# One pace instead of two for the loads of the modulation weights in the first FFN

## The chip, the cores and the metric

The kernel runs on one core of a Trainium2 chip. The metric is the device time of one execution in microseconds; the median of several executions is given. The engines are named as in the profile: PE (matrix products), DVE (vector work), ACT (activations and copies), POOL (general work) and SP, which here only issues DMA transfers. Each engine works through its own queue in order.

## The reference, cut to what matters

Two layers of a diffusion backbone run over 256 latent tokens and, as far as they are needed, 256 context tokens; the model width is 1024 and the FFN width 2816. Each sub-layer computes `x <- LayerNorm(alpha*x + w*gate*f(x*(1+scale)+shift))`. The FFN is `(silu(h@Wa) * (h@Wu)) @ Wout`. Shift, scale and gate come from nine "modulation" vectors a layer:

```python
m  = (silu(c)     @ ada_w[i] + ada_b[i])   # 9 vectors of 1024 for the latent tokens
mc = (silu(c_ctx) @ ada_w[i] + ada_b[i])   # the same for the context tokens
```

Layer 0 is FFN, neighbourhood attention, FFN; layer 1 is FFN, short convolution, FFN. All is float32.

## The kernel before, in words

Every weight matrix is loaded in units of 512 KB (256 rows by 512 columns), and each unit is split into a high part (ACT copy, line 205) and a low part (DVE subtraction, line 208). Each product is made of three matmuls (high by high, low by high, high by low), which are float32r and 512 columns wide.

The first FFN of layer 0 runs over latent and context tokens together (512 columns). Its 2816 hidden columns are worked in three parts (`parts`, of 4, 4 and 3 panels of 256). In each part come first the panels (`f0_mm`, lines 615 to 617, then silu, product and a split in `f0_gate`, lines 621, 622, 110 and 111), and then the second product of that part (`out_gemm` over `ffn_w_out`, lines 162 to 165), whose results are added to x by `residual` (lines 366 to 373).

Beside it, as background, the kernel computes the modulation vectors that later sub-layers need. `ada` loads the weights in chunks of 128 rows by 1024 columns (512 KB, line 285, three buffers `ar`) and DVE multiplies each by the conditioning column and accumulates (first chunk of a vector line 276, the others line 278). A group has two accumulators `acc` of 1024 columns, and there are two such buffers, so that the accumulation of the next group can begin only when PE has read the accumulators of the group before. PE sums over the partitions with four small matmuls (line 309), DVE adds the bias (line 310), and the rows go to DRAM (line 312). Groups 1 to 3 accumulate one vector for both kinds of tokens: 8 chunks, each used twice (four DVE instructions a chunk). Groups 4 to 7 hold two vectors for the latent tokens: 16 chunks, each used once (two DVE instructions).

`ada` is a generator: one call of it (`bg_step`) issues one chunk with its accumulation, or one of the four steps that close a group (bias, two empty ones, the small matmuls). Groups 1 to 3 so take 12 calls each, and groups 4 to 7 take 20; the small matmuls fall on the calls 12, 24, 36, 56, 76, 96 and 116. The calls are dealt out by `tick`: the rate `background[1]` is added at every tick, and each whole one is a call. A tick is six wide matmuls of PE. The first part of the FFN has 40 ticks of panels after the background is set up (rate 0.45) and 32 of second product, the second part 64 and 32, the third part 48 and 24.

The order of PE's instructions is the order of the program, written out by hand. For the other engines a list scheduler decides the order ahead of the run: by priority (place in the program, moved forward by 40 for the weight splits and back by `ADA_LATE` = 20 for the background from the second part's second product on), and by when it expects data and buffers. On the chip each queue then runs in that fixed order.

Of the kernel before, what the change touches and what calls it, by code (L numbers as in the profile page):

```python
# [68 lines left out]
def backbone_kernel(  # L69
# [23 lines left out]
    def nm(s):  # L93
        uid[0] += 1
        return f"{s}_{uid[0]}"
# [7 lines left out]
    def mmb(s="mm", t=0):  # L103
        return bank("at" if t % 2 else "mm", s)
# [11 lines left out]
    background = [None, 0.0, 0.0]  # L116
# [19 lines left out]
    def bg_step():  # L136
        with tc.high_priority(offset=-ada_late[0]):
            if next(background[0], 0) == 0:
                background[0] = None

    def tick(n=1):
        clock[0] += n
        for w in [w for w in waiting if w.due <= clock[0]]:
            w.get()
        background[2] += background[1] * n
        while background[0] is not None and background[2] >= 1:
            background[2] -= 1
            bg_step()
# [186 lines left out]
    def fold_cols(l, v, m, ln):  # L335

        r = sm.tile([32, P], F32, tag="mrow", bufs=2, name=nm("mrow"))
        for i, src in enumerate((scr[l][v, (m + 1) * D:(m + 2) * D], scr[l][v, m * D:(m + 1) * D],
                                 ln_g[ln[0], ln[1]], ln_b[ln[0], ln[1]])):
            sync.dma_start(r[8 * i:8 * i + 8], src.rearrange("(a b) -> a b", b=P))  # L340

        def rest():
            ps = tpb("mcT")
            nc.tensor.transpose(ps[:, 0:32], r, ident[0:32, 0:32])
            c = sm.tile([P, 6, KC], F32, tag="gcol", bufs=2, name=nm("gcol"))
            nc.vector.tensor_copy(c[:, 0:4].rearrange("p a b -> p (a b)"), ps[:, 0:32])
            nc.vector.scalar_tensor_tensor(out=c[:, 4], in0=c[:, 0], scalar=1.0, in1=c[:, 2], op0=ALU.add, op1=ALU.mult)
            nc.vector.scalar_tensor_tensor(out=c[:, 5], in0=c[:, 0], scalar=1.0, in1=c[:, 3], op0=ALU.add, op1=ALU.mult)
            nc.vector.tensor_tensor(out=c[:, 5], in0=c[:, 5], in1=c[:, 1], op=ALU.add)
            return c[:, 4], c[:, 5]  # L350

        return Late(6, rest)
# [9 lines left out]
    def residual(ps, xt, gate, wgt, alpha, stats=None, behind=()):  # L362

        t = sp.tile([P, 512], F32, tag="tmp", bufs=3, name=nm("res"))[:, 0:ps.shape[1]]
        with queued(behind[0:1]):
            nc.vector.scalar_tensor_tensor(out=t, in0=ps, scalar=wgt, in1=gate, op0=ALU.mult, op1=ALU.mult)
        with queued(behind[1:2]):
            if alpha is None:
                nc.vector.tensor_tensor(out=xt, in0=xt, in1=t, op=ALU.add)
            else:  # L370
                nc.vector.scalar_tensor_tensor(out=xt, in0=xt, scalar=alpha, in1=t, op0=ALU.mult, op1=ALU.add)
            if stats is not None:
                nc.vector.bn_stats(stats, xt)

    def stat_tile(n=2):
        return sm.tile([P, 3, 6], F32, tag="stats", bufs=6, name=nm("st"))[:, 0:n]

    def finish_stats(st):
        mv = sm.tile([P, 2], F32, tag="mv", bufs=6, name=nm("mv"))
        norm_ins[:] = [nc.vector.bn_aggr(mv, st)]  # L380
        rs = sm.tile([P, 1], F32, tag="rs", bufs=6, name=nm("rs"))
        nc.gpsimd.tensor_tensor(out=rs, in0=mv[:, 1:2], in1=lnc[:, 0:1], op=ALU.add)
        nc.gpsimd.tensor_tensor(out=rs, in0=rs, in1=lnc[:, 1:2], op=ALU.pow)
        return mv, rs
# [5 lines left out]
    def modulated(z, mv, rs, GB, lag, ahead=False):  # L390

        for h in range(2):
            norm_ins[1:] = [nc.vector.tensor_scalar(z[h], z[h], mv[:, 0:1], rs, op0=ALU.subtract, op1=ALU.mult)]

        def rest():
            G, B = GB.get()
            res = []
            for h in range(2):
                ps = tpb("hT")
                for k in range(4):  # L400
                    nc.tensor.transpose(ps[:, k * P:(k + 1) * P], z[h][:, k * P:(k + 1) * P], ident)
                t = sp.tile([P, 512], F32, tag="s2", bufs=S2, name=nm("h"))
                with tc.high_priority(offset=LN_EARLY):
                    hi, lo = act(F32R, "hTh"), act(F32R, "hTl")
                    for k in range(4):
                        s, c = slice(k * P, (k + 1) * P), slice(4 * h + k, 4 * h + k + 1)
                        nc.scalar.activation(t[:, s], ps[:, s], AF.Identity, bias=B[:, c], scale=G[:, c])
                    ins = split(t, hi, lo)
                res.append((hi, lo))
            if ahead:  # L410
                fence[:] = [i.ins for i in ins]
            return res

        return Late(lag, rest)
# [33 lines left out]
    def run(gen):  # L448
        for _ in gen:
            pass  # L450
# [159 lines left out]
    def f0_mm(ps, units, j, z, ks):  # L610
        s = slice(z * 256 + j * P, z * 256 + (j + 1) * P)
        for k in ks:
            hi, lo = units[k // UK]
            lh, ll = hi[:, k % UK, s], lo[:, k % UK, s]
            nc.tensor.matmul(ps, lh, hT0[k][0], start=(k == 0), stop=False)  # L615
            nc.tensor.matmul(ps, ll, hT0[k][0], start=False, stop=False)  # L616
            nc.tensor.matmul(ps, lh, hT0[k][1], start=False, stop=(k == KC - 1))  # L617

    def f0_gate(bk):
        t = sp.tile([P, 512], F32, tag="s2", bufs=S2, name=nm("sil0"))  # L620
        nc.scalar.activation(t, bk[0], AF.Silu)
        nc.vector.tensor_tensor(out=t, in0=t, in1=bk[1], op=ALU.mult)
        hi, lo = act(F32R, "gh"), act(F32R, "gl")
        split(t, hi, lo)
        return hi, lo

    def w1(p, us=range(KU)):
        return [wpair(w_in, u, p * 256, FF + p * 256, "w1") for u in us]
# [28 lines left out]
    for fh, (p0, p1) in enumerate(parts):  # L657
        gT = []
        for p in range(p0, p1):
            units = u0 if p == 0 else u1 if p == 1 else w1(p)  # L660
            for j in range(2):
                if p == 0:
                    bk = b0[j]
                elif p == 1 and j == 0:
                    bk = b1
                else:
                    bk = []
                    for z in range(2):
                        bk.append(mmb("f0", z))
                        for k in range(0, KC, 2):  # L670
                            f0_mm(bk[z], units, j, z, (k, k + 1))
                            tick()
                gT.append(f0_gate(bk))
        if fh == 0:
            for v in range(2):
                big = hp.tile([P, 2, 512], F32, tag="pt", bufs=4, name=nm("gate"))
                sync.dma_start(big.rearrange("p a b -> p (a b)"),
                               bass.AP(scr[0].tensor, scr[0][v, 2 * D:3 * D].offset, [[0, P], [1, D]]))
                gates.append([big[:, 0], big[:, 1]])
            background[1] = 0.44  # L680
        elif fh == 1:
            background[1] = 0.64
            ada_late[0] = ADA_LATE

        def evac(t, n, bank, fh=fh):
            if fh < 2:
                residual(bank, xt[t][n], gates[t // 2][n], 0.5, None if fh else ALPHA)
                return
            if n == 0:
                stats[t] = stat_tile()  # L690
            residual(bank, xt[t][n], gates[t // 2][n], 0.5, None, stats[t][:, n])
            if n == 1:
                mv, rs = finish_stats(stats[t])
                hTs[t] = modulated(xt[t], mv, rs, GB[t // 2], F0_LAG[t])

        if fh == 2:
            while made[0] < 5:
                bg_step()
            GB = [fold_cols(0, v, 3, (0, 0)) for v in range(2)]
        nk = 2 * (p1 - p0)  # L700
        order = [(t, n, u) for n in range(2) for t in range(4) for u in range(nk // UK)]
        run(out_gemm(w_out, lambda k, t: (gT[k][0][:, t * P:(t + 1) * P], gT[k][1][:, t * P:(t + 1) * P]),
                     nk, order, evac, "w2", wrow0=p0 * 256))
# [454 lines left out]
```

## Time and profile before

| | us |
|---|---|
| median of 3 executions | 1268.82 |
| the three executions | 1268.34, 1268.82, 1272.64 |
| the profiled execution | 1273.84 |
| its span, from first to last instruction | 1272.0 |
| PE busy in it | 1246.2 |
| DVE busy | 954.9 |
| ACT busy | 590.2 |
| mean granted TensorE clock | 0.995 |

The span is the time between the first and the last instruction that the profiler shows; the execution's own time is 1.84 us longer. PE's busy share is not the same as PE at its peak, but idle time of PE is time in which the program's longest engine did nothing. [...]

### The profile page before, as it was taken

The numbers are of one execution on the slowest core, as the hardware profiler recorded it, in microseconds if no ns is written. First come the engines' busy times: TensorE is split into PE (matmuls) and PEld (weight loads), VectorE is DVE, ScalarE is ACT, GpSimd is POOL, SyncE is SP. The second block draws the span as 40 slices with busy tenths as digits, with TensorE's granted clock in tenths as the row PEclk, the third lists the DMA queues.
The fourth block names the chain that finished last, engine by engine and source line by source line (L and its number), as shares of the span: only waits on it lengthen the run. The fifth ranks groups of instructions, "written<-read, shape, count | busy, mean of one in ns | idle before, by whom it ended". The sixth has DMA issues, their size and how long they took to land.

```text
span 1272.0 us, 17236 instructions
## 1 busy us (share of the span) xinstructions
PE 1246.2 (98%) x5890; PEld 1007.0 (79%) x5890; DVE 954.9 (75%) x1681; ACT 590.2 (46%) x1148; POOL 42.3 (3%) x71
## 2 busy tenths in 40 slices
PE   7999999999999999989999999999999999999997
PEld 5787778788768878767888788888788887888786
DVE  3699887688878867888898646997646787977545
ACT  2432132412315556577755435645435744655431
POOL 0000000000001111111000000000000000000000
PEclk9999999999989999999999999999999999999999
DMA  9877578587862654554899745798645764786641
GB/s 298 297 230 244 177 239 296 162 303 246 287 212 67 196 123 79 108 128 123 274 310 333 236 148 182 253 325 286 228 146 170 234 213 133 256 285 187 222 155 54
DMA packets 202712, 268.59 MB, mean 211 GB/s; under 512 B 30026, under 2 KB 149298, under 8 KB 202624
## 3 DMA queue, kind: packets, MB, share of 16 engines
q1 hardware_dynamic: 202624, 267.49, 66.3%
q8 instruction: 46, 0.75, 0.2%
q14 instruction: 42, 0.34, 0.1%
HBM read 265.27 MB, written 2.17 MB: 210 GB/s over the span
## 4 chain that ended last, share of the span: by engine, by line
PE 88%; DVE 4%; DMA 3%; ACT 3%; issue 1%; POOL 0%; SPq 0%; DVEq 0%; ACTq 0%; POOLq 0%
PE w L162 17%; PE w L165 17%; PE w L163 17%; PE f L615 6%; PE f L616 6%; PE f L617 6%; PE wc L162 2%; PE wc L165 2%; PE wc L163 2%; PE wkv L162 2%; PE wkv L163 2%; PE wkv L165 2%; PE gT L467 1%; DMA bias<-in_na_rpb_dram 1%; DMA w1r<-in_ffn_w_in_dram 1%
## 5 line engine op out<-in xcount | busy, mean ns | idle before, releaser
L205 ACT ACTIVATE w1h<-w1r 128x512 fp32r<-128x512 f32 x348 | 199.8, 624 | 172.8 <-PE w L165 51.8
L208 DVE TENSOR_TENSOR w1l<-w1r,w1h 128x512 fp32r<-128x512 f32 x348 | 223.3, 688 | 49.0 <-ACT w1h L205 47.0
L162 PE MATMUL w<-w1h,hTh 128*128 128x512 f32 x528 | 209.5, 397 | 0.9 <-ACT hTh L110 0.9
L163 PE MATMUL w<-w1l,hTh 128*128 128x512 f32 x528 | 205.9, 390 | 0.0
L278 DVE SCALAR_TENSOR_TENSOR acc<-ar,cst,acc 128x512 f32<-128x512 f32 x266 | 185.7, 749 | 15.9 <-DMA ar<-in_ada_w_dram 15.8
L162 PE MATMUL w<-w2h,gh 128*128 128x512 f32 (+1 forms) x446 | 174.8, 393 | 3.1 <-ACT gh L110 3.1
L163 PE MATMUL w<-w2l,gh 128*128 128x512 f32 (+1 forms) x446 | 173.2, 389 | 0.0
L208 DVE TENSOR_TENSOR w2l<-w2r,w2h 128x512 fp32r<-128x512 f32 x176 | 114.3, 688 | 73.5 <-ACT w2h L205 72.8
L205 ACT ACTIVATE w2h<-w2r 128x512 fp32r<-128x512 f32 x176 | 101.5, 624 | 144.9 <-PE w L165 122.1
L165 PE MATMUL w<-w1h,hTl 128*128 128x512 f32 x528 | 163.4, 391 | 0.5 <-DVE hTl L111 0.2
L615 PE MATMUL f<-h0h,w1h 128*128 128x512 f32 x352 | 139.4, 396 | 0.3 <-ACT w1h L205 0.3
L617 PE MATMUL f<-h0l,w1h 128*128 128x512 f32 x352 | 137.7, 391 | 0.0
L616 PE MATMUL f<-h0h,w1l 128*128 128x512 f32 x352 | 137.7, 391 | 0.0
L165 PE MATMUL w<-w2h,gl 128*128 128x512 f32 (+1 forms) x446 | 137.0, 389 | 0.0
L162 PEld LDWEIGHTS w<-w1h,hTh 128*128 128x128 f32 x528 | 99.2, 188 | 23.9 <-ACT hTh L110 1.7
L165 PEld LDWEIGHTS w<-w1h,hTl 128*128 128x128 f32 x528 | 98.8, 188 | 23.1 <-DVE hTl L111 2.2
L163 PEld LDWEIGHTS w<-w1l,hTh 128*128 128x128 f32 x528 | 99.3, 188 | 19.7 <-DVE w1l L208 0.2
L162 PEld LDWEIGHTS w<-w2h,gh 128*128 128x128 f32 x446 | 84.4, 189 | 22.9 <-ACT gh L110 3.5
L165 PEld LDWEIGHTS w<-w2h,gl 128*128 128x128 f32 x446 | 84.0, 189 | 17.5
L163 PEld LDWEIGHTS w<-w2l,gh 128*128 128x128 f32 x446 | 84.5, 190 | 16.7
L615 PEld LDWEIGHTS f<-h0h,w1h 128*128 128x128 f32 x352 | 66.5, 189 | 18.6 <-issue 4.6
L617 PEld LDWEIGHTS f<-h0l,w1h 128*128 128x128 f32 x352 | 66.3, 188 | 14.1 <-DVE h0l L593 0.3
(180 smaller groups left out, 1703.1 us busy)
## 6 DMA issues: line engine op xcount, KB each, us to landing
w1r<-in_ffn_w_in_dram SPq DMA_DIRECT2D x352, 256.0 KB
ar<-in_ada_w_dram SPq DMA_DIRECT2D x128, 512.0 KB
w2r<-in_ffn_w_out_dram SPq DMA_DIRECT2D x88, 512.0 KB
ar<-in_ada_w_dram SPq DMA_DIRECT2D x32, 256.0 KB
wkvr<-in_na_w_qkv_dram SPq DMA_DIRECT2D x32, 256.0 KB
wcr<-in_sc_w_in_dram SPq DMA_DIRECT2D x32, 256.0 KB
wqr<-in_na_w_qkv_dram SPq DMA_DIRECT2D x8, 512.0 KB
bias<-in_na_rpb_dram SPq DMA_DIRECT2D x64, 64.0 KB
```

Source lines behind the costliest of these rows:

```text
L162: nc.tensor.matmul(ps, lh, rh, start=first and i == 0, stop=False)
L163: nc.tensor.matmul(ps, lh, rl, start=False, stop=False)
L165: nc.tensor.matmul(ps, ll, rh, start=False, stop=last and i == n - 1)
L205: nc.scalar.activation(hi[:, a:a + m // W_HI], raw[:, a:a + m // W_HI], AF.Copy)
L208: nc.vector.tensor_tensor(out=lo[:, a:b], in0=raw[:, a:b], in1=hi[:, a:b].bitcast(F32), op=ALU.subtract)
L278: nc.vector.scalar_tensor_tensor(out=a, in0=src, scalar=sc, in1=a, op0=ALU.mult, op1=ALU.add)
L467: nc.tensor.transpose(ps[:, j * 256 + i * P:j * 256 + (i + 1) * P], g[:, j * P:(j + 1) * P], ident)
L615: nc.tensor.matmul(ps, lh, hT0[k][0], start=(k == 0), stop=False)
L616: nc.tensor.matmul(ps, ll, hT0[k][0], start=False, stop=False)
L617: nc.tensor.matmul(ps, lh, hT0[k][1], start=False, stop=(k == KC - 1))
```

## The change

The rate that is set after the first part's panels becomes 0.53 instead of 0.44, and the rate that is set after the second part's panels becomes 0.53 instead of 0.64. Nothing else is changed: the same instructions, buffers and priorities' offsets, dealt out at other places.

```diff
-            background[1] = 0.44
+            background[1] = 0.53
         elif fh == 1:
-            background[1] = 0.64
+            background[1] = 0.53
             ada_late[0] = ADA_LATE
```

## Rows read from the trace of the kernel before

**Rows 1.** The page: busy time, and the chain by engine
```profile
PE 1246.2 (98%) x5890; PEld 1007.0 (79%) x5890; DVE 954.9 (75%) x1681; ACT 590.2 (46%) x1148; POOL 42.3 (3%) x71
...
PE 88%; DVE 4%; DMA 3%; ACT 3%; issue 1%; POOL 0%; SPq 0%; DVEq 0%; ACTq 0%; POOLq 0%
```
**Rows 2.** Windows of 32 us, first FFN: PE, PEld, DVE, ACT, POOL (instructions), clock, DMA, GB/s
```profile
96.00:128.00 32.00, 32.00 (x145) 25.58 (x144) 30.87 (x50) 8.64 (x15) 0.00 (x0) 1.00 0.73 237
...
320.00:352.00 32.00, 32.00 (x145) 25.59 (x144) 26.90 (x44) 10.29 (x18) 0.00 (x0) 1.00 0.86 287
352.00:384.00 32.00, 28.92 (x118) 22.09 (x117) 21.91 (x41) 6.36 (x11) 0.00 (x0) 0.89 0.59 193
```
**Rows 3.** Timeline of PE around the idle at 366 us; in brackets idle before
```profile
363.13 0.39 PE L162 MATMUL w<-w2h,gh 128*128 128x512 f32 x1
...
369.55 0.79 PE L162 MATMUL w<-w2h,gh 128*128 128x512 f32 x1 [3.08 <-ACT gh L110]
```
**Rows 4.** Timeline of ACT, the last panel and the third second-product
```profile
367.11 1.86 ACT L205 ACTIVATE w2h<-w2r 128x512 fp32r<-128x512 f32 x3 [5.30 <-DMA w2r<-in_ffn_w_out_dram]
368.88 0.61 ACT L110 ACTIVATE gh<-sil 128x512 fp32r<-128x512 f32 x1
```
**Rows 5.** Timeline of SP's queue, 343 to 361 us
```profile
351.80 8.22 SPq L285 DMA_DIRECT2D ar<-in_ada_w_dram  x4
360.07 0.94 SPq L202 DMA_DIRECT2D w2r<-in_ffn_w_out_dram  x2
```
**Rows 6.** Timeline of DVE, 365 to 368 us
```profile
365.82 1.42 DVE L278 SCALAR_TENSOR_TENSOR acc<-ar,cst,acc 128x512 f32<-128x512 f32 x2 [1.48 <-DMA ar<-in_ada_w_dram]
...
367.75 0.68 DVE L622 TENSOR_TENSOR sil<-sil,f 128x512 f32<-128x512 f32 x1
```
**Rows 7.** Windows of 2 us behind that idle (columns as in Rows 2)
```profile
368.00:370.00 2.00, 0.45 (x1) 0.45 (x2) 2.00 (x4) 1.92 (x4) 0.00 (x0) 0.65 0.05 18
370.00:372.00 2.00, 2.00 (x6) 1.52 (x6) 2.00 (x5) 0.02 (x1) 0.00 (x0) 0.50 0.80 246
...
374.00:376.00 2.00, 2.00 (x7) 1.62 (x6) 0.10 (x1) 0.00 (x0) 0.00 (x0) 0.65 0.87 328
```
**Rows 8.** The chain in order of time: five modulation products (start, us)
```profile
98.89 0.99 PE ada L309 x8
...
136.84 1.00 PE ada L309 x8
...
174.79 1.00 PE ada L309 x8
...
286.04 1.00 PE ada L309 x8
...
329.43 0.99 PE ada L309 x8
```
**Rows 9.** Timeline of DVE, group three, 134 to 171 us
```profile
134.16 0.69 DVE L366 SCALAR_TENSOR_TENSOR res<-w,gate 128x512 f32<-128x512 f32 x1 [3.54 <-PE w L165]
...
136.23 2.65 DVE L208 TENSOR_TENSOR w2l<-w2r,w2h 128x512 fp32r<-128x512 f32 x4 [0.66 <-ACT w2h L205]
...
161.09 1.29 DVE L208 TENSOR_TENSOR w1l<-w1r,w1h 128x512 fp32r<-128x512 f32 x2
...
162.96 0.68 DVE L366 SCALAR_TENSOR_TENSOR res<-w,gate 128x512 f32<-128x512 f32 x1
...
164.82 6.05 DVE L278 SCALAR_TENSOR_TENSOR acc<-ar,cst,acc 128x512 f32<-128x512 f32 x9
```
**Rows 10.** Windows of 4 us around the shorter idle at 556 us
```profile
556.00:560.00 4.00, 2.04 (x15) 1.56 (x15) 3.51 (x8) 3.92 (x10) 0.73 (x1) 0.97 0.78 156
560.00:564.00 4.00, 4.00 (x16) 2.65 (x16) 3.59 (x9) 2.16 (x5) 1.42 (x2) 0.61 0.49 66
```
**Rows 11.** Timeline of DVE: the last accumulations of groups 4 and 6
```profile
213.30 2.74 DVE L278 SCALAR_TENSOR_TENSOR acc<-ar,cst,acc 128x512 f32<-128x512 f32 x4
...
323.54 0.75 DVE L278 SCALAR_TENSOR_TENSOR acc<-ar,cst,acc 128x512 f32<-128x512 f32 x1
```

## The prediction

> **What bounds the kernel now.** I read the page first. PE is busy for 1246.2 us of the span, and 88% of the chain that ended last is PE [rows 1]. So the change can give only what PE loses in the stretch that it touches, and it can take only by making PE wait there. The windows come next [rows 2]. From 320 to 352 us, as in the 32-us windows before it from 64 us on, PE is busy for all of the 32 us at clock 1.00. One window differs: 352 to 384, with 28.92 us busy and a clock of 0.89. DVE is the second engine to watch: 30.87 of 32 us between 96 and 128.
>
> The timelines show that one hole. The third second-product begins at 363.13; PE then stands 3.08 us before 369.55, released by the high part `gh` of the last panel's gate [rows 3]. ACT makes that `gh` at 368.88, right behind three copies of w2 units which waited 5.30 us for their transfer [rows 4]. The transfer was issued at 360.07, behind four chunks of the last modulation group that held SP's queue for 8.22 us [rows 5]. DVE has the same cause from another side: the product that `gh` is copied from starts at 367.75, behind an accumulation that waited for its chunk until 365.82 [rows 6]. So what ends last here is the tail of modulation group 7. [...] Hole and clock are 6.0 us. More than that is not to be had.
>
> **The change, part by part.** No instruction is added or removed. 116 calls of the background are dealt out at other ticks. A tick costs PE (136.84 - 98.89 - 1.0) / 27 = 1.37 us, from the first two products of line 309 [rows 8], which lie 27 ticks apart. The calls add up like this: 40 ticks at 0.45 give 18 calls in both versions. Group 2 closes on call 24: before, 6 / 0.44 = 14 ticks on, at tick 54; after, 6 / 0.53 = 12 ticks on, at 52. Group 3 closes on call 36: 18 / 0.44 = 41, tick 81; after 18 / 0.53 = 34, tick 74. In the same way group 4 goes from 127 to 112, group 5 from 161 to 150, group 6 from 192 to 188, group 7 from 224 to 225. The faster first rate and the slower second one meet at the end: 111 calls are made in both when the third second-product begins. The first 40 ticks are not touched.
>
> What counts is the distance between two closings, not the rate alone: a group's accumulation starts only when PE has read the accumulators of the one before, and PE, whose order is fixed, stands at line 309 if DVE isn't done.
>
> *Group 3, squeezed.* Before, its gate (product 2) was at 136.84 and DVE's last nine accumulations of the group ran from 164.82 for 6.05 us, to 170.87 [rows 9]: 34.0 us, in which DVE had hardly a gap. The product stood at 174.79, 3.9 us later. Now it is due 22 ticks after the gate, 22 x 1.37 + 1.0 = 31.1 us. DVE's work has not shrunk: PE would stand 34.0 - 31.1 = 2.9 us. Upper end: the gate comes at 134.1, and so a residual that DVE did before it (at 134.16, two instructions of about 0.65 us) falls behind it: 4.2. Lower end: DVE could put off two low splits of the coming panel (161.09, and the like before them: 2.6 us together) and the last residual (from 162.96, 1.3), and it stood idle for 3.54 and 0.66 us ahead of the gate [rows 9], so that work may move there: 0. I take 2.9, the plain shift. The clock comes on top: an idle of 1.96 us at 556 to 560 us was followed by a window at 0.61, 4 x 0.39 = 1.6 us lost [rows 10], and 3.08 us of idle cost 2.9. For 2.9 us I take 2.6, with ends of 0 and 4.0 (2.9 / 3.08 for each us of a 4.2 hole). Sum +5.5, ends 0 and +8.2.
>
> *Groups 4 to 6, relaxed.* All of them get 38 ticks, 53.0 us. Group 4 needed from 174.79 to 213.30 + 2.74 = 216.0, 41.3 us; group 6 from 286.04 to 324.3, 38.3 us [rows 8, 11]. Cost nothing: 11 us and more of room cover them.
>
> *Group 7, earlier.* Its gate, product 6, moves 4 ticks ahead, 5.5 us against PE's own work. Before, the chunk that DVE waited for came 365.82 - 329.43 = 36.4 us after the gate, and the w2 copies began 367.11 - 329.43 = 37.7 after it [rows 4, 6, 8]. The third second-product lay 33.7 us after the gate and will lie 39.2 after it. At the same speed both are ready 1.5 to 2.8 us ahead of it, and hole and clock go: -6.0. The other end is 0: ACT's order puts the w2 copies ahead of `gh`, so a transfer that is still late keeps the hole. Next late is the same pair, with 1.5 us to spare.
>
> The window from 320 to 352 us moved 287 GB/s at a DMA share of 0.86 [rows 2]. [...]
>
> *The queues that the calls are moved past.* Chunks move ahead of weight units on SP, which issues in order. The longest that four chunks held it is 8.22 us [rows 5]; four raw weight buffers hold a whole panel, 16 ticks or 21.9 us of PE. That covers it; with less than one panel ahead, the cost would be up to the 8.2. The write of line 312 waits on SP for product 3 as before. DVE's splits have priority over accumulations, but the order is planned ahead, and one that is wrong by 1 to 2 us somewhere is not visible from here.
>
> Sum: -6.0 + 5.5 = -0.5 us on the profiled execution, 1273.84 to 1273.3. That execution lies 5.0 us above the median, about what the hole is worth, so the faster executions may have less of it. I carry the difference over: 1268.82 - 0.5 = 1268.3.
>
> **The rivals.**
> 1. The swap above: the hole at 366 us goes, one at product 3 comes. For it: both gates are fixed by the same ticks. Likeliest. 1268.3; with its ends from -3 to +2.5 it lies in 1266 to 1271.5.
> 2. Only the gain. DVE's idle ahead of the gate and the splits that can wait take up the 2.9 us. For it: 4.2 us of idle. Against it: the idle is there because nothing else was ready. 1268.8 - 6.0 = 1262.8.
> 3. Only the loss, the slower side. Place: PE at line 309 of group 3, early in the second part's first panel. Price: 2.9 us idle and 2.6 of clock. It decides from the point at which DVE needs over 31.1 us for the group, and it stands alone if ACT still places the w2 copies ahead of `gh`. 1268.8 + 5.5 = 1274.3, at the upper end 1277.
> 4. Nothing happens. Chunks are issued whenever a buffer is free and the scheduler fills in the same order; the tail of group 7 is as late as before. For it: the group takes 36 to 38 us whatever the rate is, being bound by its buffers and transfers. Against it: its gate does move. 1268.8. [...]
>
> **How the numbers follow.** Chances: swap 0.45, gain only 0.20, loss only 0.20, nothing 0.15. Half a per cent is 6.3 us, about what a measurement of this kernel can tell from no change. The gain alone, 6.0, stops just short of it; with the spread of the executions it passes in about half its cases: faster 0.11, a little from larger gains included. The loss passes towards its upper end, about half its cases, and a misplaced order elsewhere adds 0.05: slower 0.15. The rest, 0.74, is the same. The range runs from the gain's 1262 to 1276, between the loss's middle and end.
>
> **What would show it.** In the profile after: the small products of line 309 start at 98.9, 134, 165 to 169, then 53 us apart. Group 3: idle of PE ahead of line 309, released by DVE's accumulation; right if 0 to 4 us, and the step is wrong if there is none. Around 363 us (later by that idle and its clock): `gh` straight behind the product, no idle above 1 us, clock 1.00. The w2 transfers are issued some 5 us earlier against the start of the third second-product. What would make all of it wrong: a new hole in the panels of the second or third part, released by a weight split; or groups 4 to 7 that end no earlier against their products than before. Outside the first FFN nothing should change.

## The result, and the profile after

The changed kernel takes 1272.79 us (median of 10 executions, 1271.69 to 1273.91), the kernel before 1269.38 (10 executions, 1268.13 to 1272.67): a ratio of 1.0025, with a 95% interval of 1.0016 to 1.0035. It is slower by 3.4 us, 2.0 to 4.4 by the interval. The prediction had 1268.3 us, half a microsecond faster, as its likeliest case; its rival "only the loss" had 1274.3.

The profiled execution of the changed kernel took 1272.61 us, its span 1270.8. The page: busy time, the chain by engine, and the one group of panel matmuls with notable idle time ahead of it.

```profile
PE 1246.1 (98%) x5890; PEld 1005.3 (79%) x5890; DVE 954.3 (75%) x1681; ACT 590.0 (46%) x1148; POOL 41.3 (3%) x71
...
PE 82%; DVE 9%; DMA 4%; ACT 3%; issue 1%; POOL 1%; SPq 0%; DVEq 0%; ACTq 0%; POOLq 0%
...
L616 PE MATMUL f<-h0h,w1l 128*128 128x512 f32 x352 | 138.2, 393 | 2.2 <-DVE w1l L208 2.0
```

PE is busy as long as before [rows 1], but DVE has got a share of 9% in the chain (4% before), and PE has waited 2.2 us ahead of line 616 for a low split (`w1l`, line 208).

The windows of 32 us (columns as in [rows 2]):

```profile
160.00:192.00 32.00, 29.84 (x123) 22.06 (x123) 27.84 (x46) 7.17 (x13) 0.00 (x0) 0.95 0.78 250
...
352.00:384.00 32.00, 32.00 (x145) 25.31 (x144) 24.35 (x44) 7.43 (x14) 0.00 (x0) 1.00 0.53 178
```

The hole has changed its place. From 160 to 192 us PE has lost 2.16 us and some clock (0.95 of the full clock, the window's mean); from 352 to 384 us, where the profile of before had 28.92 us at 0.89 [rows 2], nothing is lost.

PE's timeline at the new hole, and windows of 2 us around it:

```profile
164.73 0.50 PE L616 MATMUL f<-h0h,w1l 128*128 128x512 f32 x1 [2.03 <-DVE w1l L208]
```

```profile
164.00:166.00 2.00, 1.27 (x6) 1.05 (x6) 2.00 (x5) 0.00 (x0) 0.00 (x0) 1.00 0.06 11
166.00:168.00 2.00, 1.87 (x6) 0.82 (x6) 2.00 (x4) 0.00 (x0) 0.00 (x0) 0.55 0.87 281
168.00:170.00 2.00, 2.00 (x8) 0.40 (x5) 1.32 (x3) 0.00 (x0) 0.00 (x0) 0.59 0.94 261
170.00:172.00 2.00, 2.00 (x10) 1.36 (x8) 1.82 (x4) 0.00 (x0) 0.00 (x0) 1.00 1.05 364
```

PE waits 2.03 us before 164.73 for a low split of the second part's first panel, the panel that starts after the first second-product. Behind the idle time the clock is near half for two windows (0.55 and 0.59), as it was in [rows 7].

What the split waited for stands on ACT and DVE. First ACT's high copies of that panel (the first two lines are its first two units, the third its last unit), then DVE's queue:

```profile
138.75 1.15 ACT L205 ACTIVATE w1h<-w1r 128x512 fp32r<-128x512 f32 x2 [0.21 <-ACT w2h L205]
140.11 1.15 ACT L205 ACTIVATE w1h<-w1r 128x512 fp32r<-128x512 f32 x2 [0.21 <-ACT w1h L205]
...
159.15 1.16 ACT L205 ACTIVATE w1h<-w1r 128x512 fp32r<-128x512 f32 x2 [0.21 <-ACT w1h L205]
```

```profile
133.40 0.69 DVE L366 SCALAR_TENSOR_TENSOR res<-w,gate 128x512 f32<-128x512 f32 x1 [3.55 <-PE w L165]
...
147.37 4.06 DVE L278 SCALAR_TENSOR_TENSOR acc<-ar,cst,acc 128x512 f32<-128x512 f32 x6
...
160.38 1.89 DVE L208 TENSOR_TENSOR w1l<-w1r,w1h 128x512 fp32r<-128x512 f32 x3
...
163.99 2.49 DVE L208 TENSOR_TENSOR w1l<-w1r,w1h 128x512 fp32r<-128x512 f32 x4
166.40 2.73 DVE L278 SCALAR_TENSOR_TENSOR acc<-ar,cst,acc 128x512 f32<-128x512 f32 x4
```

ACT had finished the copies of the first two units by 141.3 us, and the panel's last by 160.3. DVE began the first of the eight low splits at 160.38, because between 139.7 and 160.4 its queue held 24 accumulations of line 278 (of which the rows show a group of 6) and the residuals; PE went on as the split begun at 163.99 ended. So no transfer and no copy held DVE up: the splits stood behind the accumulations. In these rows DVE kept to its queue's order: the first low split did not pass one of the 24 accumulations, though its high copy had been finished for 19 us.

The products of line 309 in the chain (the first to the fourth, and the sixth):

```profile
98.13 1.00 PE ada L309 x8
...
133.36 1.00 PE ada L309 x8
...
167.75 2.68 PE ada L309 x8
...
222.38 1.00 PE ada L309 x8
...
328.74 0.99 PE ada L309 x8
```

Product 1, which the change doesn't touch, comes 0.76 us earlier here than in [rows 8]. Counted from it, product 2 lies where the ticks put it (133.36, forecast 134.1). Product 3 was due at about 164.5. It began at 167.75 because of the hole, and it took 2.68 us instead of 1.00: the last four accumulations of its group ran in DVE's queue from 166.40 to 169.13, and PE waited for them inside the product. Product 6 is 230.6 us behind product 1, and in [rows 8] 230.5: in spite of the loss at group 3 it has kept its place, so against PE's own work it has moved ahead, as forecast.

ACT at the third second-product, for comparison with [rows 4], and PE's first matmul of it:

```profile
368.13 1.15 ACT L205 ACTIVATE w2h<-w2r 128x512 fp32r<-128x512 f32 x2 [0.20 <-ACT w2h L205]
369.36 0.63 ACT L110 ACTIVATE gh<-sil 128x512 fp32r<-128x512 f32 x1
```

```profile
367.88 0.39 PE L162 MATMUL w<-w2h,gh 128*128 128x512 f32 x1
```

The w2 copies still stand ahead of `gh`, but they don't wait for their transfer any more, and `gh` at 369.36 does not hold PE up: the window has 32.00 us busy. The third second-product begins 39.1 us after product 6 (forecast 39.2).

### The profile page after: what moved, and what is told of

Its sections match the earlier page's. It is cut to its first block, busy times and chain, and to the rows that moved or that the text cites. A ratio compares the mean times of both kernels' runs of the same rounds, so it can differ in the third digit from the quotient of the medians.

```text
span 1270.8 us, 17220 instructions
## 1 busy us (share of the span) xinstructions
PE 1246.1 (98%) x5890; PEld 1005.3 (79%) x5890; DVE 954.3 (75%) x1681; ACT 590.0 (46%) x1148; POOL 41.3 (3%) x71
## 4 chain that ended last, share of the span: by engine, by line
PE 82%; DVE 9%; DMA 4%; ACT 3%; issue 1%; POOL 1%; SPq 0%; DVEq 0%; ACTq 0%; POOLq 0%
PE w L162 15%; PE w L165 15%; PE w L163 15%; PE f L615 6%; PE f L616 6%; PE f L617 6%; PE wc L162 2%; PE wc L165 2%; PE wc L163 2%; DVE w1l L208 2%; DVE acc L278 2%; PE wkv L162 1%; DMA w1r<-in_ffn_w_in_dram 1%; PE wkv L163 1%; PE wkv L165 1%
## 5 line engine op out<-in xcount | busy, mean ns | idle before, releaser
L616 PEld LDWEIGHTS f<-h0h,w1l 128*128 128x128 f32 x352 | 66.5, 189 | 16.6 <-DVE w1l L208 3.5
```

## The experiments

Each kernel was timed in five rounds beside the kernel before on the same chip, unless it says otherwise. The ratios are to those runs of before. The letters of theories and rivals are explained in the expectations, and A means something else in the first of them; A1 and D are two readings of what is squeezed in group 3.

**The kernel before, four more profiles.** No edit. One kernel with five rounds and three single profiled executions.

> The kernel before, unchanged, looked at once more. Theory A (the hole at 366 us was in the one profiled execution of 1273.8 us but not in the usual ones of about 1269): ratio 1.000; if the profiled execution is at 1270 us or less, PE's idle around 363 to 370 us is under 1 us and no half clock follows it; if it is at 1272 us or more, the hole of about 3 us is there. Rival B (the hole is in every execution, and the changed kernel loses some 9 us in a place that its one profile does not show): the hole of 3 us is there at any time.

> The kernel before, one more profile. Theory A: its time follows the hole at 366 us: at 1270 us or less the idle there is under 1 us and the clock stays at 1.00 behind it; at 1272 us or more it is 2 us or more, with half clock behind it.

> The kernel before, one more profile, to be read as the look ahead of it: idle at 366 us against the execution's own time.

> The kernel before, one more profile, to be read as the two looks ahead of it: idle at 366 us against the execution's own time.

Measured: the first has a median of 1268.67 us over 12 executions, ratio 1.0008 (0.9994 to 1.0022); its profiled execution took 1267.59 us. The single executions took 1271.36, 1268.47 and 1269.38 us. PE's timeline around 367 us in the four, in this order (idle in brackets), with the windows of the first:

```profile
367.35 0.50 PE L162 MATMUL w<-w2h,gh 128*128 128x512 f32 x1 [0.57 <-ACT gh L110]
```

```profile
366.00:368.00 2.00, 1.43 (x7) 0.80 (x5) 1.96 (x5) 1.67 (x3) 0.00 (x0) 1.00 0.59 172
368.00:370.00 2.00, 2.00 (x10) 1.61 (x9) 2.00 (x5) 0.00 (x0) 0.00 (x0) 1.00 0.80 247
```

```profile
367.20 0.50 PE L162 MATMUL w<-w2h,gh 128*128 128x512 f32 x1 [1.13 <-ACT gh L110]
```

```profile
367.45 0.50 PE L162 MATMUL w<-w2h,gh 128*128 128x512 f32 x1 [0.61 <-ACT gh L110]
```

```profile
367.55 0.50 PE L162 MATMUL w<-w2h,gh 128*128 128x512 f32 x1 [0.98 <-ACT gh L110]
```

Idle of 0.57, 1.13, 0.61 and 0.98 us, and in the windows of the first no half clock behind it (the other three have 1.00 there too). The hole of 3.08 us with 2.9 us of clock in [rows 3, 7] belonged to one execution of 1273.84 us; these four lose about 0.8 us there. Rival B falls, and theory A stands for executions of up to 1270 us; its other half, that those of 1272 us and more have the hole, was not met again in a profile. What differed was less the hold on SP's queue than the transfer itself: from its issue to the first copy that waited for it the w2 transfer took 7.0 us in [rows 4, 5] (360.07 to 367.11), and 4.7, 5.1, 5.0 and 5.5 us in these four (in the first 360.08 to 364.80). Why is open.

The execution of 1271.36 us lies between the limits of theory A. Its lost time is elsewhere: PE stands 1.41 us before 441.49, in the attention, and the clock is near half behind it.

```profile
441.49 0.50 PE L898 MATMUL S<-kTl,qTh 64*128 64x512 f32 x2 [1.41 <-DVE kTl L111]
```

```profile
442.00:444.00 2.00, 2.00 (x7) 1.48 (x6) 1.71 (x5) 0.28 (x1) 0.00 (x0) 0.61 1.06 340
444.00:446.00 2.00, 2.00 (x7) 1.54 (x6) 0.28 (x1) 1.16 (x4) 0.00 (x0) 0.54 0.79 212
```

**Only the first rate.**

```diff
-            background[1] = 0.44
+            background[1] = 0.53
         elif fh == 1:
             background[1] = 0.64
```

> Only the first rate, 0.44 to 0.53; the second stays 0.64. Theory A (the loss is the hole at the start of the second part's panels, where the third group's accumulations stand ahead of the low splits in DVE's queue; 2 us of idle and 3 us of clock): slower by about 3.5 us, ratio 1.0025 to 1.004, with PE idle of about 2 us at 163 to 165 us released by a low split. Rival C (the loss comes from the second rate, which holds group 7 back): ratio 1.000 and no such hole.

Measured: 1272.94 us, ratio 1.0038 (1.0025 to 1.0052). PE's timeline at the hole:

```profile
165.84 0.50 PE L616 MATMUL f<-h0h,w1l 128*128 128x512 f32 x1 [2.04 <-DVE w1l L208]
```

The same hole, 2.04 us, released by a low split, at nearly the same place. The first rate alone makes the loss.

This profile also shows what the half clock was worth. Behind the hole the clock stays at 1.00 here. The window behind it, the products 2, 3 and 4 in the chain, and DVE's last accumulations of group 3:

```profile
168.00:170.00 2.00, 1.98 (x7) 0.41 (x6) 2.00 (x4) 0.00 (x0) 0.00 (x0) 1.00 0.96 304
```

```profile
134.48 0.99 PE ada L309 x8
...
168.40 2.94 PE ada L309 x8
...
223.24 0.99 PE ada L309 x8
```

```profile
167.51 2.74 DVE L278 SCALAR_TENSOR_TENSOR acc<-ar,cst,acc 128x512 f32<-128x512 f32 x4
```

From product 2 to product 4 it takes 88.76 us at full clock, and 222.38 - 133.36 = 89.02 us in the changed kernel with its two windows near half clock. So the slow clock cost only some 0.3 us there. In both profiles DVE ends the group's accumulations 35.8 us after product 2 (170.25 and 169.13), and PE, fast or slow, stands inside product 3 until then.

**Only the second rate.**

```diff
             background[1] = 0.44
         elif fh == 1:
-            background[1] = 0.64
+            background[1] = 0.53
```

> Only the second rate, 0.64 to 0.53; the first stays 0.44. Theory A: no hole at 160 to 180 us, ratio 0.999 to 1.001. Rival C: slower by 3 us or more, ratio 1.0025, with idle of PE around the third second-product or behind it, where group 7 now ends (its product moves from tick 224 to the end of the FFN).

Measured: 1271.90 us, ratio 1.0029 (1.0015 to 1.0042). That is a miss for theory A, which had no change: there is no hole at 160 to 180 us, as it said, but the kernel is slower. PE's idle time from 384 us on, and product 7 in the chain:

```profile
404.32 0.66 PE L401 MATMUL hT<-ident,xc 128*128 128x128 f32 x4 [1.60 <-ACT h L407]
...
443.50 0.50 PE L898 MATMUL S<-kTl,qTh 64*128 64x512 f32 x2 [2.52 <-DVE kTl L111]
```

```profile
398.32 1.00 PE ada L309 x8
```

Product 7 now falls at 398.32, into the first work of the attention, with 1.60 us of idle at 404 us and 2.52 at 443 us. Rival C describes this kernel, but not the change: there the two rates together bring product 7 back to 380.75 us. The two losses don't add up (1.0038 and 1.0029 alone, 1.0025 together), since the slower second rate costs only if the first has not given it a lead. That the two idle pieces come from the accumulations that now run beside the layer norm is what the order suggests; it was not tried, and the execution of before at 1271.36 us has a smaller piece (1.41 us) at the same line 898. Behind the idle time of 2.52 us the clock stays at 1.00:

```profile
444.00:446.00 2.00, 2.00 (x12) 1.54 (x9) 1.71 (x5) 0.27 (x1) 0.00 (x0) 1.00 1.04 360
```

**Product 3 later.** The changed kernel with three empty calls more in group 3. All calls of the later groups come three later too.

```diff
-        yield 1
+        yield from [1] * (4 if vecs[0][:2] == (0, 4) else 1)
```

> The changed kernel with three more empty calls ahead of the third group's small product, so that it falls on tick 80 instead of 74; chunks and accumulations stay where the change put them. Theory A1 (PE waits for low splits that stand behind some twenty accumulations in DVE's queue; the product's own date doesn't matter): the hole of about 2 us at a low split at 163 to 165 us stays, ratio 1.002 to 1.004. Rival D (as the prediction had it: the closer date of product 3 is what squeezes): the hole goes, ratio 0.999 to 1.001.

Measured: 1271.53 us, ratio 1.0013 (1.0001 to 1.0024). PE's timeline, windows of 2 us behind the hole, and products 2 and 3 in the chain:

```profile
164.29 0.80 PE L616 MATMUL f<-h0h,w1l 128*128 128x512 f32 x1 [2.03 <-DVE w1l L208]
```

```profile
164.00:166.00 2.00, 1.71 (x4) 1.43 (x5) 2.00 (x5) 0.00 (x0) 0.00 (x0) 0.56 0.24 45
166.00:168.00 2.00, 2.00 (x7) 1.54 (x7) 2.00 (x5) 0.00 (x0) 0.00 (x0) 0.59 0.97 299
```

```profile
132.92 1.00 PE ada L309 x8
...
176.11 1.00 PE ada L309 x8
```

The hole at the split is there, 2.03 us, though product 3 now comes only at 176.11. So the date of the product is not what PE waits for first. The ratio is lower than theory A1 gave (1.002 to 1.004; only the upper end of the interval reaches into that), and still on the slower side: product 3 itself takes 1.00 us again, so the second wait of the changed kernel is gone.

**Splits first.** The changed kernel with the second part's first panel further forward.

```diff
-            units = u0 if p == 0 else u1 if p == 1 else w1(p)
+            w_early[0] = 90 if p == 4 else W_EARLY; units = u0 if p == 0 else u1 if p == 1 else w1(p)
```

> The changed kernel with the weight units of the second part's first panel moved further forward in priority (90 instead of 40), so that DVE's queue has their low splits ahead of the last accumulations of group 3. Theory A1 alone: no hole at all, ratio 0.999 to 1.001. Rival D: the hole only moves to the four small matmuls of product 3, which now wait 2 to 4 us for the accumulations, with the clock behind it: ratio 1.002 to 1.004. Rival E (transfer or high copy of these units is late): the hole stays at the low split.

Measured: 1273.85 us, ratio 1.0033 (1.0020 to 1.0047). PE's timeline:

```profile
168.63 3.81 PE L309 MATMUL ada<-acc,ones 128*32 128x512 f32 x8 [2.89 <-DVE acc L278]
```

The split is in time, and now the four small matmuls of product 3 wait 2.89 us for the accumulations, and then take 3.81 us instead of 1.00. This is the hole that the prediction had described, in its place; that the first wait has the forecast size of 2.9 us is chance, since PE waits on inside the product. The change itself met DVE's lateness one step earlier, at the split. Theory A1 alone and rival E fall, D stands behind A1.

**Both.** The two edits above together.

> The changed kernel with both of the edits: splits further forward and product 3 at tick 80. If DVE's work of group 3 has to be done either before the first panel's splits or before product 3 (A1 and D together): PE has no hole of over 0.5 us between 150 and 200 us, ratio 0.998 to 1.001. Rival F (the loss of the change has another place): ratio 1.0025 all the same.

Measured: 1267.32 us, ratio 0.9985 (0.9975 to 0.9995). Windows, and products 2 and 3 in the chain:

```profile
160.00:192.00 32.00, 32.00 (x146) 25.56 (x145) 26.89 (x43) 10.93 (x19) 0.00 (x0) 1.00 0.77 246
...
352.00:384.00 32.00, 32.00 (x142) 26.02 (x140) 29.20 (x53) 9.94 (x17) 0.00 (x0) 1.00 0.65 223
```

```profile
134.10 0.99 PE ada L309 x8
...
173.41 1.00 PE ada L309 x8
```

No hole from 160 to 192 us and none at the end of the FFN. With both waits lifted, the pace of 0.53 is as good as the kernel before and a little better. Rival F falls. Products 2 and 3 lie 39.31 us apart here, and 43.19 with product 3 later alone, with the same ticks between them: there, where PE had other work behind the hole, the 2.03 us of idle cost 3.9 us, nearly all of the rest being the slow clock.

**Less work for DVE.** The changed kernel leaves out 14 of the 32 accumulations of group 3: the context's vector takes the first chunk alone. The loads stay.

```diff
-                    if vec[:2] != (l, m):
+                    if vec[:2] != (l, m) or (vec == (0, 4, 1) and k > 0):
                         continue
```

> The changed kernel without 14 of the 32 accumulations of group 3 (the context vector takes the first chunk alone): 9 us less work for DVE between products 2 and 3, the loads unchanged. If DVE's work is what the change squeezes (A1 or D): no hole at 150 to 200 us, ratio 0.998 to 1.001. Rival G (the loads of the chunks or of the weights, which come in the same numbers, are late): the hole stays, ratio 1.002 to 1.004.

Measured: 1267.50 us, ratio 0.9990 (0.9979 to 1.0001). The products 2 and 4 in the chain:

```profile
132.96 0.99 PE ada L309 x8
...
217.01 1.01 PE ada L309 x8
```

No hole (PE is busy for 32.00 us from 160 to 192 us), with the same loads at the same pace: what is squeezed is DVE's work, not the transfers, and rival G falls. This kernel also prices the squeeze. From product 2 to product 4 it takes 217.01 - 132.96 = 84.05 us; the changed kernel takes 89.02. The squeeze costs 5.0 us, the waits at the split and in product 3 together (4.7 at full clock, with the first rate alone).

**Another place for the second rate.** 0.44 until group 3 is closed, then one pace for groups 4 to 7: 0.56, and in a second kernel 0.60.

```diff
-            made[0] += 1
+            made[0] += 1; background[1] = 0.56 if made[0] == 3 else background[1]
...
             background[1] = 0.44
         elif fh == 1:
-            background[1] = 0.64
+            background[1] = 0.56
```

> 0.44 until the third group is closed, then one pace of 0.56 for groups 4 to 7: group 3 is not squeezed, and the gates of groups 4 to 7 are evenly spaced. Theory A: no hole at 160 to 180 us and none at 366 us, in no execution: 1268 to 1269 us, ratio 0.998 to 1.000, and fewer executions at 1272 us. Rival C: as slow as the changed kernel, 1.0025.

> As the kernel with 0.44 until group 3 is closed, but 0.60 instead of 0.56 from there: product 7 moves from tick 225 to about 217, at the start of the third second-product, and the other gates move ahead with it. If the 1.1 us of idle that was left at 367 us came from the tail of group 7: under 0.3 us there, 1266 to 1267 us, ratio 0.997 to 0.999. Rival: the accumulations crowd the splits elsewhere, a new hole, ratio 1.000 to 1.003.

Measured: with 0.56, 1267.12 us, ratio 0.9982 (0.9967 to 0.9996), the slowest of 11 executions at 1268.74; with 0.60, 1266.66 us, ratio 0.9983 (0.9974 to 0.9992). Windows of the one with 0.56, and the last of them of the one with 0.60:

```profile
160.00:192.00 32.00, 32.00 (x145) 25.58 (x144) 28.01 (x45) 10.83 (x19) 0.00 (x0) 1.00 0.74 243
...
352.00:384.00 32.00, 30.73 (x137) 23.61 (x136) 25.13 (x47) 9.64 (x17) 0.00 (x0) 1.00 0.46 157
```

```profile
352.00:384.00 32.00, 32.00 (x146) 25.29 (x145) 23.11 (x44) 9.94 (x17) 0.00 (x0) 1.00 0.44 138
```

Group 3 keeps its room, and the hole at 160 to 192 us isn't there. With 0.56, 1.27 us are still lost at the third second-product (theory A had none), with 0.60 nothing. Both are faster than the kernel before and the changed one; between the two, the runs don't tell.

## Why the prediction was wrong

**The step that failed: "Group 7, earlier ... hole and clock go: -6.0".** The mechanism was right. Product 6 moved ahead, the w2 copies no longer waited, and in the profile after the idle at the third second-product is gone. The size was wrong, because its term came from an execution that is not the usual one. The four further profiles of before have 0.57 to 1.13 us of idle there and no half clock: the term is about -0.8 us, not -6.0. The two kernels in which the pace of 0.53 stays and group 3 has no wait bear this out within their noise: "both" is 1.9 us faster than before (0.6 to 3.2), "less work for DVE" 1.3 us (2.7 faster to 0.1 slower). The 2.9 us of clock in the -6.0 are what the windows of that one execution lose against 1.00 [rows 7]: 0.2 on 0.45 us busy at 0.65, 2.0 on two windows of 2 us at 0.50 (370 to 374 us), and 0.7 on one at 0.65; the four further profiles have 1.00 in all of these windows. The prediction saw that the profiled execution lay 5.0 us above the median and said that this was "about what the hole is worth", and then carried the difference over all the same. The two readings lead to different forecasts: with -0.8 the sum is +4.7 us, 1273.5, close to the rival "only the loss" (1274.3).

**Group 3, squeezed: +5.5, nearly right in size, and partly by luck.** Measured 5.0 us. The reason, too much work for DVE between products 2 and 3, is shown by the kernel with less of it, and the lower rate up to product 3 removes it. The parts were wrong both ways. DVE needed 35.8 us from product 2, not 34.0, against the 31.1 that PE left it: 4.7 us, not 2.9. Most of the difference is what the prediction had for its upper end (4.2): the residual at 133.40 now falls behind product 2. The clock was given 2.6 us and cost some 0.3, because it was added to a wait that does not depend on it: the first rate alone lost 4.7 us at full clock.

The place was one step off too. The prediction had PE wait at line 309; in the changed kernel the low splits of the next panel come first, behind 24 accumulations in DVE's queue (2.03 us), and the rest of the wait is inside product 3. For the lower end of its range the prediction had let DVE put off four of those splits at no cost, when it was such splits that PE needed first.

**Groups 4 to 6, relaxed: nothing, as forecast.** With both waits of group 3 lifted there is no loss left at the pace of 0.53. In the changed kernel itself PE loses 0.21 us between 256 and 288 us, where the kernel before lost nothing.

**The sum.** -0.8 + 5.0 = +4.2 us; measured +3.4, with 2.0 to 4.4 inside the interval. The ends that the prediction gave its likeliest case, -3 to +2.5, don't follow from its own terms, which add up to -6.0 and +2.2; the forecast doesn't hang on them. The rest of the kernel was to stay as it was, and in the profile the windows behind the first FFN are like those of before. The gain was near 0 because the stall is absent from the usual execution. The 287 GB/s of the window from 320 to 352 us, which the prediction names [rows 2], is close to the most that such windows show up to 384 us in the profiles before and after: 299 and 307, both from 0 to 32 us.

**Of the rivals**, "only the loss" came nearest, though not by the reason that it gave (ACT's order still placing the w2 copies ahead of `gh`): the gain did come, but there was little to gain.

## What to carry to other kernels

A stall that is found in one profile is a term of the sum only if the usual execution has it: when the profiled execution lies above the median by about the stall's worth, take the stall as absent and keep it as an end of the range, or look at more profiles first. Idle time and the slow clock behind it may be added only where the engine has work to do behind the stall (here 2.03 us of idle cost 3.9 us with its clock); where it runs into a second wait for the same late engine, that wait takes up what the clock cost (here all but some 0.3 us of it). When background work on an engine gets a closer date, ask not only whether it will be done by then, but what the engine's queue now holds behind it: the first loser is whatever waits in that queue with the nearest need (here the low splits behind 24 accumulations, 2.03 us of idle on PE). A rate of background work can follow the stretch's own room: here 0.44 while each chunk costs DVE four instructions and 0.56 or 0.60 once it costs two beat the kernel before by 0.2%. One pace of 0.53 did as well once the two waits of group 3 were lifted.

## What the runs showed of the hardware that was not expected

The length of an idle piece did not settle what the clock did behind it. In these profiles 2.03 us of idle on PE (changed kernel, 164.7 us, and with product 3 later, 164.3 us) was followed by two windows of 2 us near half clock, but 2.04 us at the same place with the first rate alone was followed by full clock. So was 2.52 us with the second rate alone (443 us), while 1.41 us in one execution of before (441 us) was followed by near half. What decided is not shown.

Nor is the price of a hole fixed: 2.03 us of idle with its slow clock cost 3.9 us where PE had other work behind it, and of the 5.0 us at group 3 in the changed kernel the clock made some 0.3.

The same program's small race between a transfer and a queue (w2 copies ahead of `gh`) left PE idle for 0.57 to 3.08 us in five profiles of identical code, with the transfer taking 4.7 to 7.0 us from its issue to the copy.
